# Five modulation rows moved into the up projection's loop, and a pause ahead of row 39

## The chip, the core and the metric

One core of a Trainium2 chip runs the whole kernel as one program. The core has a matrix engine (TensorE, PE in the profile, with its weight loads as PEld), a vector engine (VectorE, DVE), a scalar engine (ScalarE, ACT), GpSimd (POOL) and a queue that issues transfers (SyncE, SP); GpSimd issues transfers too. The metric is the device time of one execution, in us.

## The reference

Two groups of tokens go through one layer of a diffusion backbone: 128 context tokens and 512 latent tokens, 640 columns in all, with a model width of 1024.

```python
def trunk_layer(x, cvec, lw, ...):
    mod = jax.nn.silu(cvec) @ lw['w_ada'] + lw['b_ada']
    sh1, sc1, g1, sh2, sc2, g2 = jnp.split(mod, 6, axis=-1)
    h = rmsnorm(x, lw['norm1_g']) * (1.0 + sc1) + sh1
    mix, kh, vh, s_f, s_b = token_mixers(h, lw, ...)
    x = x + g1 * mix
    h = rmsnorm(x, lw['norm2_g']) * (1.0 + sc2) + sh2
    x = x + g2 * conv_ffn(h, lw['w_up'], lw['ffn_conv_w'], lw['ffn_conv_b'], lw['w_down'])

def conv_ffn(h, w_up, cw, cb, w_down):
    z = dwconv3(h @ w_up, cw, cb)
    a, g = jnp.split(z, 2, axis=-1)
    return (jax.nn.silu(g) * a) @ w_down
```

`mod` has 6 x 1024 entries for each of two condition vectors (c for the latent tokens, c_ctx for the context). In tiles of 128 these are 48 rows: 0 to 15 are sh1 and sc1, 16 to 23 g1, 24 to 39 sh2 and sc2, 40 to 47 g2. The token mixers hold a gated convolution, a recurrence, a neighbourhood attention over windows of keys with softmax, and a gated MLP.

## The kernel before

The program is one straight line of stages: the input projections (tile by tile, with the mixers' steps running beside them), the gates and branch products, the output projection, the second norm, the up projection (22 pairs of column tiles) and the down projection (42 units). Large products are made in float32 with a high and a low part of each operand, three matmuls of 320 columns for one, and with a Strassen-like scheme of seven products for a block of four.

**The modulation rows.** Rows 0 to 15 are made with matmuls at the start. The others are made on the vector engine without TensorE: a row's weights (128 x 1024, 512 KB from `w_adt`) are multiplied with silu(c) and silu(c_ctx), which stand spread over all partitions in the buffer S0, and summed along the row. `col_products` gives these two instructions (L285, one for each vector; the first writes its products to `junk`, the second over the weights). `modulate` (L234) or `gain_col` (L291) adds the bias. `ada_cols` is a job that does this for rows 16 to 41 beside the projections; it takes turns with the mixers' jobs by planned times, each `yield` naming planned us until its next step. Even rows are loaded into the buffer H, odd ones into X0 or A (in the attention's stage: A). The load of a row is asked for ahead of the products of the row before it, or behind its first product.

**The attention's stage.** `attn` goes over 16 units (head pair, column block, head) in rounds of two. `s1` makes the scores of two units on TensorE (L841, L844), adds bias and mask (L848), takes the maxima (L850), and ScalarE makes the exponentials (L851). `s2` scales by the reciprocal sums on the vector engine (L857, L858) and transposes the scores on TensorE (L861) into B (copied by the vector or the scalar engine). `s3` multiplies with the values (L878). Between these steps TensorE works on the input projection's tiles (L375). What stands in which order on each engine follows from the planned times; at run time each engine goes through its instructions in order.

**The up projection.** `up_all` calls `up_pair` for each pair p. Its instructions stand on each engine in the order of the code (`ovec`, `oact`, `opool` keep it). In a pair the vector engine does: the convolution's taps of an older pair, differences into `ubuf`, the low part of the next pair's first weights (`up_al`), `first_sum`, the gated product, the weight sums of the next pair (`up_sums`, out of the weights' buffers raw and G), taps, the last difference of the pair before, and low parts of the weight sums (`up_bl`). The weights of pair p+2 are asked for in pair p. TensorE makes seven products of 12 matmuls (L1512), 84 in a pair.

**The down projection.** `down_start(u)` opens unit u: it asks for parts of the activations that the up projection has left in memory (A, B, C, D, E, F), makes some of the modulation rows (`col_make` by the table `COLS`), and in unit 26 turns g2's columns into rows (`gain_rows`), which are read back into S0. `col_open`, behind the up loop, loads and activates the condition vectors again and asks for rows 42 and 43. Transfers made by `sync` keep the order in which the code asks for them.

The table of the rows in the down projection, and the settings of `ada_cols` (the last entry is the first row that it does not make):

```python
AE = (("fb", 1), 0.5, 0.5, 42)
...
COLS = dict(zip((23, 21, 19, 9, 6, 3), range(47, 39, -1)))
```

So before, rows 42, 43, 44, 45, 46 and 47 are made in units 3, 6, 9, 19, 21 and 23.

Of the kernel before, what the change touches and what calls it, by code (L numbers as in the profile page):

```python
# [12 lines left out]
AF = mybir.ActivationFunctionType  # L13
ALU = mybir.AluOpType
AX = mybir.AxisListType

P = 128
HY = 5
AE = (("fb", 1), 0.5, 0.5, 42)
COLWAIT = {}  # L20
HD = [4, 5, 2.1, 7, 2.2, 1.4, 1.5, 5, 2.0, 2, 11]
NPAIR = 22
NK = NPAIR // 2
BRIDGE = 4
# [26 lines left out]
D = 1024  # L51
# [10 lines left out]
C_C, C_BADA, C_N1, C_N2 = 0, 16, 64, 72  # L62
# [8 lines left out]
def tile_step(ctx: ExitStack, tc: tile.TileContext, a: dict, outs: list, dbg=None):  # L71
# [58 lines left out]
    def region(tag, shape, dt=F32):  # L130
        return big.tile(shape, dt, tag=tag, name=nm(tag))
# [24 lines left out]
    act, mm = Ordered(nc.scalar, boot).activation, ten.matmul  # L156
# [121 lines left out]
    def col_products(f, raw, cr):  # L278
        junk = gp.tile([P, D], mybir.dt.bfloat16, tag="gt", name=nm("junk"))
        ar = sp.tile([P, 2], F32, tag="red", name=nm("ar"))  # L280

        def steps():
            for v in range(2):
                tc.keep_in_program_order(
                    vec.scalar_tensor_tensor(raw if v else junk, raw, 1.0, cr[:, v], ALU.mult, ALU.mult,  # L285
                                             accum_out=ar[:, v:v + 1]))
                yield v
        return ar, steps()

    def gain_col(f, ar):  # L290
        vec.tensor_scalar(gcol[:, f // 8 // 5, :, f % 8], ar, p1[:, C_BADA + f:C_BADA + f + 1], None, ALU.add)  # L291

    def col_home(f):

# [1107 lines left out]
    def up_al(p_, raw):  # L1402
        w = up[p_, "A"]
        ovec.tensor_tensor(w[:, 2:4], raw, w[:, 0:2].bitcast(F32), ALU.subtract)
# [209 lines left out]
    def up_pair(p_, r):  # L1614


        n, q, o = p_ + 1, p_ - 1, p_ - 2
        inner, nx = p_ < NPAIR, n < NPAIR
        if p_ == 0:
            up_u2(p_)  # L1620
            up_back(1, "C", unit(1, 2), 5, 5, True)
            operand3()
        if o >= 0:
            taps(o, 1)
        if q >= 0:

            oact(tmp(2), up[q, "b"][0], AF.Copy)
            if p_ == 1:
                up_u2(p_)
            for (i0, i1, c) in S2:  # L1630
                ovec.tensor_tensor(ubuf(q, 1)[:, c:c + i1 - i0], up[q, "b"][1][:, i0:i1], tmp(2)[:, i0:i1],
                                  ALU.subtract)
        if nx and n >= BRIDGE:
            up_ah(n, r[n][0])
            up_al(n, r[n][0])
        if inner and p_ >= BRIDGE:
            up_start(p_)
            first_sum(p_)
        if o >= 0:
            gate(o)  # L1640
            gated(o)
        if nx and p_:
            up_sums(n, r[n], 0)
            up_sums(n, r[n], 1)
        elif p_ == NPAIR - 1:
            x_load("E")
            ld[UP + 2] = units[UP + 2][0]()
        if inner and p_ > 1:
            up_c(p_, r[p_])
        if o >= 0:  # L1650
            keep(o)
        if inner:
            if p_ + 2 < NPAIR:
                r[p_ + 2] = up_load(p_ + 2)
            elif p_ + 2 == NPAIR:
                ld[UP + 1] = units[UP + 1][0]()
        if q >= 0:

            c1 = up[q, "b"][0]
            prod(c1, q, 4, False)  # L1660
            for (i0, i1, c) in S2:
                oact(ubuf(q, 0)[:, c:c + i1 - i0], c1[:, i0:i1], AF.Copy)
            centre(q, 0)
            if p_ > 1:
                taps(q, 0)
        if inner and p_ > 1:
            up_u2(p_)
        if q >= 0:

            prod(up[q, "b"][1], q, 3, False)  # L1670
            ovec.tensor_tensor(ubuf(q, 1)[:, 1:1 + HC], up[q, "b"][1], tmp(q % 2), ALU.subtract)
            if p_ == 1:
                taps(q, 0)
                first_copy(3)
                first_sum(3)
        if nx and p_:
            up_b(n)
        if q >= 0:
            centre(q, 1)
        if nx and p_:  # L1680
            up_bl(n)
        if inner:
            b1, b2 = up[p_, "b"]
            prod(b2, p_, 5, True)
            prod(b1, p_, 7, False)
        if p_ == NPAIR - 1:
            x_load("C")
            rd[UP + 1] = units[UP + 1][1](ld[UP + 1])
            ld[UP + 3] = units[UP + 3][0]()
# [38 lines left out]
    def up_all(_):  # L1728
        fx["x"] = {1: (hh[0][:, 0], hh[0][:, 1]), 2: (hh[0][:, 2], hh[0][:, 3])}
        up_back(2, "A", unit(2, 0), 0, 4)  # L1730
        up_back(3, "A", unit(3, 0), 1, 4)
        up_back(0, "B", unit(0, 1), 2, 5)
        up_back(1, "B", unit(1, 1), 4, 5)
        drain(lambda: "n2_2" in R)
        for p_ in range(BRIDGE):
            up_start(p_)
            if p_ == 1:
                drain(lambda: "n2_3" in R)
                operands(0, 192)
        drain(lambda: "n2_4" in R)  # L1740
        r = {}
        up_back(0, "C", unit(0, 2), 3, 5)
        operands(192, HC)
        operands57()
        for p_ in range(NPAIR + 1):
            up_pair(p_, r)
        fixed[0] = False
        taps(NPAIR - 1, 1)
        gate(NPAIR - 1)
        gated(NPAIR - 1)  # L1750
        keep(NPAIR - 1)
        col_open()

    units.append((lambda: None, lambda pr: None, up_all))


# [18 lines left out]
    def x_load(tag, part=None):  # L1775

        if tag == "C":
            xr["C"] = region("C", [P, 2560])
            xr["p", 0] = xr["C"][:, 0:NK * P].rearrange("p (k t) -> p k t", t=P)
            sync(xr["p", 0], actp[0])  # L1780
            x_tail(0, 0)
        elif tag == "F":
            xr["F"] = region("F", [P, 2560])
            xr["p", 1] = xr["F"][:, D:D + NK * P].rearrange("p (k t) -> p k t", t=P)
            sync(xr["p", 1], actp[1])
            sync(xr["F"][:, 0:D], a["final_norm_g"].partition_broadcast(P))
        else:
            h, c = XR[tag]
            if (h, c) not in xr:
                xr[h, c] = region(tag, [P, 10, 256])  # L1790
            ks = slice(0, 10) if part is None else slice(5 * part, 5 * part + 5)
            sync(xr[h, c][:, ks], actx[h, c][:, ks])
            if part == 1:
                x_tail(h, c)

    def x_tail(h, c):
        o = NK * P + 256 * tail_of[h, c]
        xr["t", h, c] = xr["C"][:, o:o + 256].unsqueeze(1)
        sync(xr["t", h, c], actx[h, c][:, 10:11])
# [61 lines left out]
    hold = []  # L1861

    LAST = range(AE[3], 48)
    cols = {}

    def col_open():
        cols["c"] = region("S0", [P, 2, D])
        cf = cols["c"].rearrange("p v c -> p (v c)")
        sync(cf, a["cc"].rearrange("v c -> (v c)").partition_broadcast(P))
        keep_(act(cf, cf, AF.Silu))  # L1870
        for f in LAST[0:2]:
            col_load(f)

    def col_load(f):
        if f in LAST:
            cols[f] = region("HG"[f % 2], [P, D])
            sync(cols[f], a["w_adt"][f - 16])

    def col_make(f):
# [4 lines left out]
            pass  # L1884
        gain_col(f, ar[0])

    COLS = dict(zip((23, 21, 19, 9, 6, 3), range(47, 39, -1)))
    G2 = 27

    def down_start(u):  # L1890
        ph, j = DOWN[u]
        if u == 0:
            acc["b1"], acc["b2"] = [pm(), pm()], [pm(), pm()]
            g0, g1 = pg(), pg()
            acc["p"], acc["q"], acc["b3"] = g0[:, 0, :], g0[:, 1, :], [g1[:, 0, :], g1[:, 1, :]]
            r = region("XL1", [P, 5, 512])
            acc["c1"], acc["u2"], acc["cp"] = [r[:, 0], r[:, 1]], [r[:, 2], r[:, 3]], r[:, 4]
        for tag, part in {0: (("A", 0), ("B", 0)), 2: (("A", 1), ("B", 1)), 6: (("D", 0),), 8: (("D", 1),),
                          10: (("F", None),)}.get(u, ()):
            x_load(tag, part)  # L1900
        if u == 12:
            x2[2:4] = [x2r("X1")[:, 0:1024], x2r("X1")[:, 1024:2048]]
        if u - 2 in COLS:
            col_load(COLS[u - 2] + 2)
        if u in COLS:
            col_make(COLS[u])
        if u == G2 - 1:
            gain_rows(1)
        if u == G2:
            grows["g2"] = gain_load(1, "S0")  # L1910
            x2[4] = x2r("G")[:, 0:1024]
            r = region("H", [P, 2, 512])
            acc["u3"] = [r[:, 0], r[:, 1]]
        if u == 28:
            x2[0:2] = [x2r("X0")[:, 0:1024], x2r("X0")[:, 1024:2048]]
        for f in LATER.get((ph, j), ()):
            f()
# [493 lines left out]
```

## Time and profile before

| | us |
|---|---|
| runs: median of 3 (lowest, highest) | 1016.45 (1016.23, 1018.08) |
| the profiled execution's own time | 1015.32 |
| its span, first to last instruction | 1013.2 |
| busy: TensorE, vector engine, scalar engine, GpSimd | 993.9, 823.8, 559.4, 168.6 |
| attention's stage in the span | about 210 to 290 |
| up projection's loop | about 600 to 870 |
| down projection | about 866 to 1005, last matmul done at 1004.9 |

A line of a timeline has the start, the time, the engine, the source line, the operation, out<-in by the program's names and the shapes, a count, and in brackets how long the engine was idle ahead of it and what ended that. The page's slices are 25.3 us each; a digit is the busy share in tenths. A line of the waits names who waited, for whom, the us in total, how often, and the longest. A window's line gives the busy time and the number of instructions of each engine, the clock that was granted to TensorE, the share of the transfer engines that was busy, and GB/s.

### The profile page before, as it was taken

How to read it: one execution, taken by the hardware profiler on the slowest of the kernel's cores; microseconds unless marked ns; L12 is line 12 of the kernel's file. 1: busy time of each engine (PE TensorE's matmuls, PEld its weight loads, DVE VectorE, ACT ScalarE, POOL GpSimd, SP SyncE). 2: the span in 40 equal slices, each digit the busy share in tenths (PEclk: the TensorE clock that was granted, in tenths of full speed). 3: DMA queues.
4: the chain of work that ended last, by engine and by line, in shares of the span. 5: the costliest groups of instructions: out<-in, count | busy, mean ns of one | idle time of the engine just before them, and what ended most of it. 6: DMA issues, size and time to landing. Idle time of an engine off the chain costs nothing. (4 is left out here: it accounts for less than half of the span.)

```text
span 1013.2 us, 18951 instructions
## 1 busy us (share of the span) xinstructions
PE 993.9 (98%) x7503; PEld 941.4 (93%) x7503; DVE 823.8 (81%) x1381; ACT 559.4 (55%) x983; POOL 168.6 (17%) x223
## 2 busy tenths in 40 slices
PE   8999999997999999999999999999999999999996
PEld 6899999997999999999998899999999999888885
DVE  6778899867775667677778778998888887999897
ACT  6642343343464445444445376777777777756563
POOL 1000020322220122241010021222222222100013
PEclk9999999999999999999999999999999999999999
DMA  9875344596576399799249774766555666996462
GB/s 355 327 255 162 104 148 126 146 265 198 130 216 242 120 276 184 271 281 209 94 145 338 306 267 139 198 169 151 152 151 151 156 155 186 378 353 234 158 247 104
DMA packets 70010, 208.93 MB, mean 206 GB/s; under 512 B 9633, under 2 KB 24769, under 8 KB 67233
## 3 DMA queue, kind: packets, MB, share of 16 engines
q1 hardware_dynamic: 43536, 148.60, 41.2%
q0 software_dynamic: 26384, 59.12, 25.5%
q8 instruction: 59, 0.97, 0.4%
q14 instruction: 31, 0.25, 0.1%
HBM read 165.99 MB, written 48.51 MB: 212 GB/s over the span
## 5 line engine op out<-in xcount | busy, mean ns | idle before, releaser
L375 PE MATMUL g<-XH,w 128*128 128x320 f32 x704 | 171.7, 318 | 0.1
L375 PEld LDWEIGHTS g<-XH,w 128*128 128x128 f32 x704 | 121.2, 189 | 2.7 <-issue 1.0
L375 PE MATMUL g<-XL,w 128*128 128x320 f32 x352 | 109.0, 310 | 0.0
L375 PEld LDWEIGHTS g<-XL,w 128*128 128x128 f32 x352 | 66.6, 189 | 0.0
L1943 PE MATMUL m<-w,XH 128*128 128x512 f32 x246 | 58.6, 390 | 0.0
L1943 PEld LDWEIGHTS m<-w,XH 128*128 128x128 f32 x246 | 46.1, 188 | 9.7
L1152 PE MATMUL m<-XH,w 128*128 128x320 f32 x224 | 52.5, 309 | 0.0
L151 POOL DMA_DIRECT2D wsum<-in_w_dn_dram x36 | 36.5, 1154 | 53.0 <-issue 41.7
L151 ACT ACTIVATE w<-raw 128x1024 fp32r<-128x1024 f32 (+3 forms) x46 | 38.5, 852 | 2.3 <-DMA raw<-in_w_in_dram 1.1
L151 DVE SCALAR_TENSOR_TENSOR X<-MG,p2t,X 128x641 f32<-128x641 f32 x44 | 38.9, 884 | 1.1 <-ACT X L151 0.2
L151 DVE SCALAR_TENSOR_TENSOR X<-X,p2t,X 128x641 f32<-128x641 f32 x44 | 38.9, 884 | 1.0
L1512 PE MATMUL g<-XL,w 128*128 128x320 f32 x240 | 38.7, 310 | 0.0
L1152 PEld LDWEIGHTS m<-XH,w 128*128 128x128 f32 x224 | 38.3, 188 | 0.0
L1512 PE MATMUL g<-XL,C 128*128 128x320 f32 x240 | 38.3, 309 | 0.0
L1512 PEld LDWEIGHTS g<-XL,w 128*128 128x128 f32 x240 | 36.0, 188 | 0.6 <-ACT MG L151 0.3
L1512 PEld LDWEIGHTS g<-XL,C 128*128 128x128 f32 x240 | 36.0, 188 | 0.0
L1152 PE MATMUL m<-XL,w 128*128 128x320 f32 x112 | 34.6, 309 | 0.0
L151 ACT ACTIVATE ga<-m,cst 128x320 f32<-128x320 f32 x27 | 14.3, 528 | 36.6 <-PE m L1152 36.6
L151 DVE TENSOR_TENSOR w<-raw,w 128x1024 fp32r<-128x1024 f32 (+2 forms) x36 | 30.6, 871 | 2.5 <-ACT w L151 2.5
L151 ACT ACTIVATE X<-g 128x320 f32<-128x320 f32 x30 | 13.1, 437 | 34.6 <-PE g L1512 34.5
L1858 DVE TENSOR_TENSOR w<-raw,w 128x1024 fp32r<-128x1024 f32 (+1 forms) x26 | 30.1, 1156 | 2.5 <-ACT w L1854 2.5
L151 DVE TENSOR_TENSOR gb<-g,gb 128x640 f32<-128x640 f32 x12 | 9.9, 825 | 26.3 <-PE g L1165 25.4
(582 smaller groups left out, 2929.8 us busy)
## 6 DMA issues: line engine op xcount, KB each, us to landing
wsum<-in_w_dn_dram POOLq DMA_DIRECT2D x30, 512.0 KB, 11.7
raw<-in_w_up_dram SPq DMA_DIRECT2D x30, 512.0 KB, 5.5
raw<-in_w_gp_dram SPq DMA_DIRECT2D x21, 640.0 KB, 6.6
raw<-in_w_in_dram SPq DMA_DIRECT2D x19, 512.0 KB, 4.5
H<-in_w_adt_dram SPq DMA_DIRECT2D x16, 512.0 KB, 4.5
raw<-wsum SPq DMA_DIRECT2D x12, 512.0 KB, 5.3
actx<-X POOLq DMA_DIRECT2D x22, 256.0 KB, 4.4
wsum<-wsum POOLq DMA_DIRECT2D x10, 512.0 KB, 11.1
```

Of the source, the lines that this page charges most:

```text
L151: r = f(*args, **kw)
L375: mm(o, w[:, h, k0 + k, :], r(k)[:, s], start=(k == 0 and i == 0), stop=(k == kt - 1 and i == 2))
L1152: mm(o, w[:, k, :], x[:, k, :], start=(first and k == 0 and j == 0), stop=(k == 3 and j == 2), skip_group_check=True)
L1512: z = mm(o, w[:, k, :], x[:, k, :], start=(first and k == 0 and j == 0), stop=(k == 3 and j == 2), skip_group_check=True)
L1858: vec.tensor_tensor(w[:, 1, 0:n], raw, w[:, 0, 0:n].bitcast(F32), ALU.subtract)
L1943: mm(ps, s[t // 4][:, hx, k, o:o + P], w[:, hw, k, c0:c1], start=first, stop=i == 2 and bi == len(batch) - 1 and k == len(ks) - 1, skip_gr ...
```

## The change

`ada_cols` makes rows 16 to 39 only, and pauses for 8 planned us ahead of row 39. Rows 40 to 44 are made in the up loop: `up_row` puts one product into a pair, behind `up_al` and ahead of the pair's first products; a row's first product stands in pair 6, 9, 12, 15 or 18, its second with the bias in the pair after it. `col_open` moves from behind the loop to the start of pair 4, and the Silu of the condition vectors to pair 6. The next row's load is asked for behind a row's second product. Rows 45, 46 and 47 stay in units 19, 21 and 23 of the down projection. There, D is asked for in units 9 and 11 (was 6 and 8), F in 13 (was 10), a part of the second norm's input in 16 (was 12), and the last piece of B's part in 5 (was 2).

```diff
-AE = (("fb", 1), 0.5, 0.5, 42)
-COLWAIT = {}
+AE = (("fb", 1), 0.5, 0.5, 40)
+COLWAIT = {39: 8}
...
+        if p_ == BRIDGE:
+            col_open()
...
             up_al(n, r[n][0])
+            up_row(p_)
...
         keep(NPAIR - 1)
-        col_open()
...
-            if part == 1:
+            if part == 1 and tag != "B":
                 x_tail(h, c)
...
     LAST = range(AE[3], 48)
+    UPROWS = dict(zip((6, 9, 12, 15, 18), LAST))
     cols = {}
+
+    def up_row(p_):
+        if p_ in UPROWS:
+            f = UPROWS[p_]
+            if f == LAST[0]:
+                cf = cols["c"].rearrange("p v c -> p (v c)")
+                keep_(act(cf, cf, AF.Silu))
+            cols["job"] = (f,) + col_products(f, cols.pop(f), cols["c"])
+        if "job" in cols:
+            f, ar, steps = cols["job"]
+            if next(steps) == 1:
+                keep_(gain_col(f, ar))
+                del cols["job"]
+                if f + 1 in LAST:
+                    col_load(f + 1)

     def col_open():
         cols["c"] = region("S0", [P, 2, D])
         cf = cols["c"].rearrange("p v c -> p (v c)")
         sync(cf, a["cc"].rearrange("v c -> (v c)").partition_broadcast(P))
-        keep_(act(cf, cf, AF.Silu))
-        for f in LAST[0:2]:
-            col_load(f)
+        col_load(LAST[0])

     def col_load(f):
         if f in LAST:
-            cols[f] = region("HG"[f % 2], [P, D])
+            cols[f] = region("G" if f == 46 else "H", [P, D])
             sync(cols[f], a["w_adt"][f - 16])
...
-    COLS = dict(zip((23, 21, 19, 9, 6, 3), range(47, 39, -1)))
+    COLS = dict(zip((23, 21, 19), range(47, 44, -1)))
...
-        for tag, part in {0: (("A", 0), ("B", 0)), 2: (("A", 1), ("B", 1)), 6: (("D", 0),), 8: (("D", 1),),
-                          10: (("F", None),)}.get(u, ()):
+        for tag, part in {0: (("A", 0), ("B", 0)), 2: (("A", 1), ("B", 1)), 9: (("D", 0),), 11: (("D", 1),),
+                          13: (("F", None),)}.get(u, ()):
             x_load(tag, part)
-        if u == 12:
+        if u == 5:
+            x_tail(1, 1)
+        if u == 16:
             x2[2:4] = [x2r("X1")[:, 0:1024], x2r("X1")[:, 1024:2048]]
-        if u - 2 in COLS:
-            col_load(COLS[u - 2] + 2)
+        if u + 2 in COLS and COLS[u + 2] > 45:
+            col_load(COLS[u + 2])
```

On the vector engine in the attention's stage, before: row 38's end (modt), then row 39's first product (out of A), then the scaling of round 0's scores (ast holds the sums, X the scores, m a bank of TensorE's results).

```order
L234 TENSOR_SCALAR modt<-ar_2940,bada_240,cst 128x2
L285 SCALAR_TENSOR_TENSOR junk_2997,ar_2998<-A_2357,S_82_887 128x1024
L857 RECIPROCAL ast_2876<-ast_2876 128x1 x2
L858 TENSOR_SCALAR X_252_2814<-X_252_2814,ast_2876 128x384 x2
L848 TENSOR_TENSOR X_253_2815<-m_3007,B_2816 128x384
L848 TENSOR_TENSOR X_253_2815<-m_3009,B_2816 128x384
L850 TENSOR_REDUCE ast_2876<-X_253_2815 128x1 x2
L285 SCALAR_TENSOR_TENSOR A_2357,ar_2998<-A_2357,S_82_887 128x1024
```

The same place of the changed kernel, from row 38's end on:

```order
L234 TENSOR_SCALAR modt<-ar_2940,bada_240,cst 128x2
L857 RECIPROCAL ast_2876<-ast_2876 128x1
L858 TENSOR_SCALAR X_252_2814<-X_252_2814,ast_2876 128x384
L857 RECIPROCAL ast_2876<-ast_2876 128x1
L858 TENSOR_SCALAR X_252_2814<-X_252_2814,ast_2876 128x384
L848 TENSOR_TENSOR X_253_2815<-m_3002,B_2816 128x384
L848 TENSOR_TENSOR X_253_2815<-m_3004,B_2816 128x384
L850 TENSOR_REDUCE ast_2876<-X_253_2815 128x1 x2
```

And a little later, where row 39 now stands:

```order
L848 TENSOR_TENSOR X_252_2814<-m_3083,B_2816 128x384
L848 TENSOR_TENSOR X_252_2814<-m_3085,B_2816 128x384
L850 TENSOR_REDUCE ast_2876<-X_252_2814 128x1 x2
L285 SCALAR_TENSOR_TENSOR junk_3100,ar_3101<-A_2357,S_82_887 128x1024
L2137 COPY B_2816<-m_3111 128x384
L285 SCALAR_TENSOR_TENSOR A_2357,ar_3101<-A_2357,S_82_887 128x1024
```

Row 39's first product has moved from ahead of the scaling of the first round's scores to behind the maxima of the third round's, one scaling and two score rounds later. Rows 40 and 41, which followed it, are gone from this stage.

On the vector engine in the up loop, pair 7 of the changed kernel, around row 40's second product (MG<-raw is `up_al`, MG<-m,s is `first_sum`; before, these two stand next to each other):

```order
L151 TENSOR_TENSOR X_617_6754<-g_7311,X_616_6740 128x128
L151 TENSOR_TENSOR MG_663_7437<-raw_7354,MG_663_7437 128x1024
L285 SCALAR_TENSOR_TENSOR H_7039,ar_7309<-H_7039,S_635_7037 128x1024
L291 TENSOR_SCALAR gcol<-ar_7309,cst 128x2
L151 TENSOR_TENSOR MG_597_6559<-m_7459,s_666_7457 128x320
L151 TENSOR_TENSOR X_616_6740<-X_616_6740 128x641
```

A product, and in each second of these pairs the bias, now stand between the low part of the weights and `first_sum`.

On the SP queue of the changed kernel, row 41's load and its neighbours in the same pair (before, the weight loads follow each other without it):

```order
L1384 DMA raw_7356<-in_w_up_dram 128x1024
L1384 DMA raw_7487<-in_w_up_dram 128x1024
L1761 DMA H_7442<-in_w_adt_dram 128x1024
L1384 DMA G_7489<-in_w_up_dram 128x1024
L1384 DMA raw_7616<-in_w_up_dram 128x1024
```

The row's load has come between two halves of a pair's weights, so the second half's load and all later ones stand behind it. TensorE's own order is the same in both kernels but for two matmuls at one place in the bridge to the down projection.

More of the change, by code (lines that the diff above doesn't have):

```diff
@@ L290, in gain_col @@
     def gain_col(f, ar):
-        vec.tensor_scalar(gcol[:, f // 8 // 5, :, f % 8], ar, p1[:, C_BADA + f:C_BADA + f + 1], None, ALU.add)
+        return vec.tensor_scalar(gcol[:, f // 8 // 5, :, f % 8], ar, p1[:, C_BADA + f:C_BADA + f + 1], None, ALU.add)
     def col_home(f):
```

## The prediction

> **What bounds the kernel now.** I read the busy line and the slices of the page, then the waits of TensorE, then windows and timelines around the one wait that counts.
>
> ```profile
> PE 993.9 (98%) x7503; PEld 941.4 (93%) x7503; DVE 823.8 (81%) x1381; ACT 559.4 (55%) x983; POOL 168.6 (17%) x223
> PE   8999999997999999999999999999999999999996
> PE m L861 <- DVE X L858: 5.7, 1, 5.7
> DVE junk L285 <- DMA A<-in_w_adt_dram: 7.6, 1, 7.6
> ```
>
> TensorE is busy 993.9 of 1013.2 us, so 19.3 us are left. Between start and end only one slice is below 9, the tenth (228 to 253 us), and the third line is its cause: TensorE waited 5.7 us once, for the vector engine's softmax scaling (L858). The fourth says what the vector engine was doing then: it stood 7.6 us in front of a modulation product (L285) whose weight row had not landed. The timelines show both, with the load:
>
> ```profile
> 228.40 0.31 PE L375 MATMUL g<-XH,w 128*128 128x320 f32 x1
> 234.44 1.51 PE L861 MATMUL m<-cst,X 128*128 128x128 f32 x6 [5.73 <-DVE X L858]
> 242.64 0.82 PE L861 MATMUL m<-cst,X 128*128 128x128 f32 x6
> 249.55 0.82 PE L861 MATMUL m<-cst,X 128*128 128x128 f32 x6
> ...
> 224.69 0.28 DVE L234 TENSOR_SCALAR modt<-ar,bada,cst 128x2 f32<-128x2 f32 x1
> 232.53 1.23 DVE L285 SCALAR_TENSOR_TENSOR junk<-A,S 128x1024 bf16<-128x1024 f32 x1 [7.56 <-DMA A<-in_w_adt_dram]
> 233.68 0.22 DVE L857 RECIPROCAL ast<-ast 128x1 f32<-128x1 f32 x2
> 233.88 0.75 DVE L858 TENSOR_SCALAR X<-X,ast 128x384 f32<-128x384 f32 x2
> ...
> A<-in_w_adt_dram SPq DMA_DIRECT2D x1, 512.0 KB, 10.8
> ```
>
> Rows of w_adt go into H (even) and A (odd), so this A is row 39; the modt of 224.69 closes row 38. The load took 10.8 us to land and the vector engine, in order, could not start the scaling behind it. The scaling itself was ready: its exponentials had ended before 226 us (ACT row below). The windows show what went with the stall:
>
> ```profile
> core 0: us, PE busy (x) PEld busy (x) DVE busy (x) ACT busy (x) POOL busy (x), PEclk, DMA share, GB/s
> 225.00:228.50 3.50, 3.50 (x27) 3.08 (x25) 0.00 (x0) 2.23 (x6) 0.00 (x0) 1.00 0.99 348
> 228.50:234.50 6.00, 0.27 (x3) 0.09 (x2) 1.97 (x6) 0.14 (x1) 0.00 (x0) 0.94 0.91 356
> 234.50:237.50 3.00, 3.00 (x14) 3.00 (x15) 3.00 (x6) 1.45 (x5) 1.41 (x2) 0.55 0.02 7
> 242.60:249.60 7.00, 7.00 (x59) 6.46 (x58) 7.00 (x18) 3.86 (x8) 1.93 (x4) 1.00 0.67 188
> 640.00:850.00 210.00, 210.00 (x1434) 210.00 (x1433) 189.22 (x279) 152.66 (x263) 55.21 (x72) 1.00 0.63 159
> 900.00:925.00 25.00, 25.00 (x112) 20.69 (x111) 25.00 (x44) 13.66 (x21) 0.00 (x0) 1.00 0.91 337
> ```
>
> The transfers ran at 356 GB/s until the row landed, and after the wait the granted clock was 0.55 for three us. In the up projection (640 to 850) and the down projection (900 to 925) TensorE has no gap at all: there the other engines' loads are not the bound.
>
> **The pause ahead of row 39.** It takes row 39's first product from its place ahead of round 0's scaling to behind the maxima of the third score round. Nothing else moves ahead of the scaling, so the stall at L861 goes if the chain without row 39 is in time. For the stalled transposes it is:
>
> ```profile
> 225.53 0.19 ACT L851 ACTIVATION_READ_ACCUMULATOR X<-X,ast 128x1 f32 x1
> 225.93 0.39 PE L844 MATMUL m<-B,F 64*128 64x128 f32 x4
> 234.54 1.02 DVE L848 TENSOR_TENSOR X<-m,B 128x384 f32<-128x384 f32 x2
> 235.47 1.00 DVE L850 TENSOR_REDUCE ast<-X 128x1 f32<-128x384 f32 x2
> 240.91 0.39 PE L844 MATMUL m<-B,F 64*128 64x128 f32 x4
> 237.17 0.19 ACT L851 ACTIVATION_READ_ACCUMULATOR X<-X,ast 128x1 f32 x1
> ```
>
> The exponentials end at 225.72; reciprocals and scalings (0.22 and 0.75, some 0.95 back to back) give 226.7, and TensorE gets there at 228.7. Saved: 5.73 us. The wait also cost clock: from L861 to L861 a step takes 249.55 - 242.64 = 6.91 us, but the step behind the stall took 242.64 - 234.44 = 8.20, so 1.29 us more. In sum 7.0 us.
>
> The Trainium skill ("TensorE: Matmul & The Clock Gate", What's actually happening) says that an idle window of about 3.4 us drops the clock to half, and that a busy one of that length brings it back. The trace's 0.55 after a 5.73 us gap agrees in kind. By that rule a cold window would cost half of 3.4, 1.7 us as an estimate, and the sum would be 7.4 instead of 7.0; the measured 1.29 decides.
>
> What is late next? The following transposes come 6.91 us later, at 235.6. Their scores are out of TensorE at 226.3; sums and maxima (1.02 and 1.00) end at 228.3; the two exponentials ended 0.9 us behind their maxima (237.36 against 236.47), so at 229.2; the scalings at 230.2: 5.4 us to spare. Row 39 now stands behind the third round's maxima. Those scores ended at 241.3 and come 7.0 us earlier, at 234.3, so their maxima end at 236.3. The row landed at 232.5 in the old order, and the load of row 40, issued behind it, is gone. So 3.8 us to spare there, and I take the residual wait as zero. Its bounds are 0 and the whole 5.73.
>
> **Rows 40 and 41 leave the attention.** Four products and two loads fewer. The window 242.6 to 249.6 has the vector engine full (7.00 of 7.00) and TensorE full as well, so the relief is worth nothing to the end; it covers the products of row 39 that come into that stretch.
>
> **Rows 40 to 44 in the up loop.** One product per pair in pairs 6, 7, 9, 10 up to 19, on the vector engine's fixed order, between a pair's weight remainder and its first sum.
>
> ```profile
> 218.00 1.22 DVE L285 SCALAR_TENSOR_TENSOR junk<-H,S 128x1024 bf16<-128x1024 f32 x1
> 219.15 0.08 DVE L285 DVE_READ_ACCUMULATOR junk<-H,S 128x1 f32 x1
> 944.42 0.21 DVE L291 TENSOR_SCALAR gcol<-ar,cst 128x2 f32<-128x2 f32 x1
> ...
> 694.80 1.23 DVE L151 TENSOR_TENSOR w<-raw,w 128x1024 fp32r<-128x1024 f32 x1 [0.35 <-ACT w L151]
> 696.97 0.49 DVE L151 TENSOR_TENSOR MG<-m,s 128x320 f32<-128x320 f32 x1 [0.95 <-PE m L1512]
> 698.11 0.69 DVE L151 TENSOR_TENSOR F<-raw,G 128x512 f32<-128x512 f32 x1
> 702.37 0.48 DVE L151 TENSOR_TENSOR X<-g,X 128x320 f32<-128x320 f32 x1
> ...
> 705.50 1.92 PE L1512 MATMUL g<-XH,w 128*128 128x320 f32 x12
> 690.28 0.33 SPq L1384 DMA_DIRECT2D G<-in_w_up_dram  x1
> DMA to landing us min/median/max: 3.8/3.9/5.5
> ```
>
> A product takes 1.15 us of the queue (218.00 to 219.15), a second product with its gain 1.15 + 0.21 = 1.36. Exactly where it is put the vector engine waits 0.95 us for TensorE. So first_sum comes 0.20 us late in a pair with a first product and 0.41 in one with a second; at the next weight remainder 0.35 us of waiting are free, and each third pair has no product. The lag does not build up. What does TensorE need soonest from behind it? The bank pair that X<-g at 702.37 empties, done at 702.85, and TensorE writes it again at 705.50: 2.65 us against a lag of 0.41. Cost: none; at the other end, if every late first_sum reached TensorE, five times 0.20 + 0.41, 3.1 us. The opening Silu (1.90 us on the scalar engine in the old place) falls once into pair 6, where it delays that first_sum's copy by less than the same 2.65.
>
> The loads of rows 41 to 45 wait on the SP queue for the product that frees H, and the loads of the up weights stand behind them. That product comes at about the place of 696.97 in its pair; the G load behind it, issued at 690.28 when its buffer came free, belongs to the pair before the one of 696.97; a pair's 84 matmuls take 84 x 210/1434 = 12.3 us, so that pair's place is 684.7, 5.6 us ahead of the issue, and the row load holds nothing up. It lands in 3.9 (at most 5.5) and is read at 698.11, 7.83 after the issue: 2.3 to 3.9 us to spare. The Trainium skill ("DMA: Bandwidth & Descriptors", Queues, rings and completion order) says that each engine takes turns between the rows it has work for, packet by packet. By that, an estimate, the GpSimd transfer that frees G could take twice its time beside a row load, and the lag would grow by some tenths of a us. No row here shows the two together; it speaks for the second rival below.
>
> **Down projection.** Rows 42 to 44 leave units 3, 6 and 9, and the loads of D and F are asked for three units later. TensorE is full there (25.00 of 25.00), so the freed 3 x 2.51 = 7.5 us of the vector engine give nothing. The loads:
>
> ```profile
> 900.38 0.39 SPq L1760 DMA_DIRECT2D XL<-wsum  x1
> D<-actx SPq DMA_DIRECT2D x2, 640.0 KB, 6.3
> 929.25 2.88 PE L1943 MATMUL g<-MG,XH 128*128 128x512 f32 x12
> 1003.63 1.24 PE L1943 MATMUL m<-w,MG 128*128 128x256 f32 x9
> ```
>
> D now stands behind the weight load of 900.38 and lands near 908; its first products are those of 929.25. The stretch behind the last matmul, 1004.9 to 1013.2, is untouched.
>
> **The sum.** The profiled execution took 1015.3 us, 2.1 more than its span. Less 7.0 that is 1008.3. The median of the runs, 1016.45, stands 1.1 above it, so I forecast 1016.45 - 7.0 = 1009.4 us.
>
> **Rivals.**
> - Part of the stall comes back: row 39, or a transpose whose spare time I overrate, makes TensorE wait some 3 us a step or two later. For it: the vector engine was full in that stretch; against it: rows 40 and 41 are gone. A gap of 3 us leaves 4.0 saved, 1012.4; if it comes back whole (the pause then only carries the wait along), nothing is saved. By the Trainium skill's clock rule (the page named above) a gap under 3.4 us would cost no cold stretch on top. Chance 0.12, of which 0.03 for the whole.
> - Slower: in the up loop the vector engine becomes the bound. Five rows take 5 x (1.15 + 1.36) = 12.6 us; if all of it came onto TensorE's path the time is 1009.4 + 12.6 = 1022. It decides from a lag above 2.65 us on, and the kernel is slower once more than 7.0 of the 12.6 are exposed. For it: 189.22 of 210 us are busy there already. Against it: the free 0.95 + 0.35 us in each pair. Chance 0.07.
> - The later loads of D or F hold the down projection up. They would have to land some 20 us later than worked out; one exposed D load costs 6.3 us, 1015.7. Chance 0.03.
>
> **How the numbers follow.** The forecast has 0.78, the partial return 0.09, the whole one 0.03, the slower case 0.07, the late loads 0.03. A measurement of this kernel tells about 0.2%, 2 us, from no change. Faster: 0.78 + 0.09 = 0.87; within 0.2%: the whole return and the exposed D load, 0.06; slower: 0.07. The range reaches up to the partial return (1012.4) and the exposed first_sums (1009.4 + 3.1 = 1012.5), so to 1012.6. Downwards the fastest run of before, 1016.23, gives 1009.2; of TensorE's 19.3 idle us 5.7 go here and 8.3 lie behind the last matmul, and I leave one us of the other 5.3 for what the attention's relief may give: 1008.2.
>
> **What would show it.** Right: no wait of TensorE at L861, a granted clock of 1.00 from 225 to 240, L861 to L861 steps of 6.91 us from the first on; row 39's product starting without a DMA wait; in the up loop 1434 matmuls in 210 us as now, with first_sum's wait for TensorE gone in the pairs with a product; the last matmul 7 us earlier and the same 8.3 us behind it. Wrong: a DMA wait in front of row 39 at its new place, a gap in TensorE's row between 640 and 850, or a wait for D or F behind 920.

## The result, and the profile after

The changed kernel takes 1008.58 us (median of 4 runs, 1008.12 to 1009.04), the kernel before 1016.66 beside it (4 runs, 1016.23 to 1018.08): a ratio of 0.992, 95% interval 0.9904 to 0.9935. The forecast was 1009.4, range 1008.2 to 1012.6. The profiled execution took 1008.12 us, its span is 1006.0.

The page's busy line and TensorE's slices, then the longest row of TensorE's waits, of the changed kernel:

```profile
PE 993.2 (99%) x7503; PEld 941.0 (94%) x7503; DVE 825.0 (82%) x1381; ACT 558.5 (56%) x983; POOL 168.4 (17%) x223
PE   8999999999999999999999999999999999999996
PE g L151 <- DVE F L151: 1.6, 1, 1.6
```

The same work (993.2 us) stands in a span that is 7.2 us shorter. The 7 in the tenth slice is gone, and the longest wait that is left is one of 1.6 us, which the kernel before has as well. The windows over the place of the old stall, and the up projection:

```profile
228.50:234.50 6.00, 6.00 (x52) 5.47 (x50) 2.18 (x7) 2.88 (x8) 0.89 (x1) 1.00 1.04 334
234.50:237.50 3.00, 3.00 (x24) 2.99 (x23) 3.00 (x7) 1.78 (x6) 1.42 (x2) 1.00 0.24 46
640.00:850.00 210.00, 210.00 (x1434) 210.00 (x1433) 198.24 (x302) 151.43 (x259) 52.16 (x68) 1.00 0.66 178
```

TensorE is full at a clock of 1.00 where it stood for 5.73 us and then ran at 0.55. The up loop makes the same 1434 matmuls in 210 us, with 9 us more of work on the vector engine. Timelines of TensorE, the vector engine and SP around row 39:

```profile
228.50 0.82 PE L861 MATMUL m<-cst,X 128*128 128x128 f32 x6
...
235.40 0.82 PE L861 MATMUL m<-cst,X 128*128 128x128 f32 x6
...
242.31 0.82 PE L861 MATMUL m<-cst,X 128*128 128x128 f32 x6
...
225.90 0.42 DVE L858 TENSOR_SCALAR X<-X,ast 128x384 f32<-128x384 f32 x1
236.00 1.29 DVE L285 SCALAR_TENSOR_TENSOR junk<-A,S 128x1024 bf16<-128x1024 f32 x1
A<-in_w_adt_dram SPq DMA_DIRECT2D x1, 512.0 KB, 10.1
222.68 1.04 SPq L251 DMA_DIRECT2D A<-in_w_adt_dram  x1
```

The scaling of 225.90 no longer stands behind row 39. That row's load, issued at 222.68, lands 10.1 us later, at 232.8, and its product starts at 236.00 with no wait. The step from transposes to transposes is 6.9 us from the first on. Where the gain arises can be read off three landmarks of TensorE: the last start of L878 (the attention's products with the values), and the first and the last start of one form of L1512 (the up projection). Before, and then in the changed kernel:

```profile
L878 PE MATMUL m<-B,X x64: 272/273/324, 239.6 to 287.9; 128*64 128x128 f32 x64
L1512 PE MATMUL g<-XL,C x240: 309/309/309, 617.8 to 862.0; 128*128 128x320 f32 x120
```

```profile
L878 PE MATMUL m<-B,X x64: 272/273/323, 232.3 to 280.6; 128*64 128x128 f32 x64
L1512 PE MATMUL g<-XL,C x240: 309/309/309, 610.6 to 854.8; 128*128 128x320 f32 x120
```

So 7.3 us are won by the end of the attention, 7.2 at the up projection's start and 7.2 at its end. The last matmul ends at 997.6 instead of 1004.9, again 7.3. What lies behind the attention gives or takes nothing.

### The profile page after: what moved, and what is told of

The parts are those of the page before. It is cut to its first block, busy times and chain, and to the rows that moved or that the text cites. A ratio compares the mean times of both kernels' runs of the same rounds, so it can differ in the third digit from the quotient of the medians.

```text
span 1006.0 us, 18962 instructions
## 1 busy us (share of the span) xinstructions
PE 993.2 (99%) x7503; PEld 941.0 (94%) x7503; DVE 825.0 (82%) x1381; ACT 558.5 (56%) x983; POOL 168.4 (17%) x223
## 5 line engine op out<-in xcount | busy, mean ns | idle before, releaser
L1512 PE MATMUL g<-XL,w 128*128 128x320 f32 x240 | 38.6, 310 | 0.0
L1512 PE MATMUL g<-XL,C 128*128 128x320 f32 x240 | 38.3, 309 | 0.0
L1512 PEld LDWEIGHTS g<-XL,w 128*128 128x128 f32 x240 | 36.0, 188 | 0.6 <-ACT MG L151 0.3
L1512 PEld LDWEIGHTS g<-XL,C 128*128 128x128 f32 x240 | 36.0, 188 | 0.0
L336 ACT ACTIVATE w<-raw 128x1024 fp32r<-128x1024 f32 (+1 forms) x22 | 24.3, 1104 | 12.2 <-PE m L947 8.2
```

Source lines behind the costliest of these rows:

```text
L336: high = lambda: act(w[:, 0], raw, AF.Copy)
L1512: z = mm(o, w[:, k, :], x[:, k, :], start=(first and k == 0 and j == 0), stop=(k == 3 and j == 2), skip_group_check=True)
```

## Experiments

**The two halves alone.** The pause alone is the kernel before with `COLWAIT = {39: 8}`:

> The kernel before with the 8 us pause ahead of row 39 and nothing else; rows 40 and 41 stay in the attention's stage, 42 to 44 in the down projection. Theory (the whole gain is the stall of TensorE behind row 39, 5.7 us, and the low clock after it, 1.3 us): about 1009.5 us, L861 to L861 steps of 6.91 us. Rival (the gain needs rows 40 to 44 out of the attention and the down projection): 1013 to 1017 us.

Measured: 1010.55 us (1009.88 to 1011.30) against 1016.20, ratio 0.9945 (0.9931 to 0.9960). The rest is the changed kernel with `COLWAIT = {}`:

> The changed kernel without the pause. Theory: row 39 stands ahead of the scaling again and its load lands no earlier, so the stall of 5 to 6 us and the clock after it are back: about 1015.5 us. Rival (the move of the rows brings the gain, because row 40's load no longer crowds row 39's): 1009 to 1011 us.

Measured: 1016.99 us (1015.54 to 1018.81, 10 runs), ratio 1.0010 (1.0001 to 1.0019). The waits of TensorE in it:

```profile
PE m L861 <- DVE X L858: 6.0, 1, 6.0
```

The old stall stands whole, so moving the rows brings nothing by itself. But the pause alone is some 2 us short of the whole change (1007.8 us of span in its trace, against 1006.0): the two halves are worth more together than apart. TensorE of the pause alone runs within 0.2 us of the changed kernel up to 259 us, and then (TensorE, and the vector engine ahead of it):

```profile
260.61 0.94 PE L861 MATMUL m<-cst,X 128*128 128x128 f32 x6 [0.33 <-DVE X L858]
264.84 0.88 PE L861 MATMUL m<-cst,X 128*128 128x128 f32 x6
...
250.66 1.29 DVE L285 SCALAR_TENSOR_TENSOR junk<-A,S 128x1024 bf16<-128x1024 f32 x1
253.07 1.21 DVE L285 SCALAR_TENSOR_TENSOR A<-A,S 128x1024 f32<-128x1024 f32 x1
256.19 1.00 DVE L722 SCALAR_TENSOR_TENSOR MG<-MG,cst 128x511 f32<-128x511 f32 x2
260.14 0.74 DVE L858 TENSOR_SCALAR X<-X,ast 128x384 f32<-128x384 f32 x2
```

The pause pushes rows 40 and 41 along with row 39. Row 41's two products (2.5 us) now fall into the round in which the vector engine also does a convolution's taps (L718 to L722). That round's scaling is done only at 260.9. The planned order has laid its transposes behind that, at 260.61 where the changed kernel has them at 256.12, and from 262.2 on only the attention's own short matmuls stand between them and the next. The next transposes come at 264.84, in the changed kernel at 263.03: 1.8 us late, and the last start of L878 is 1.8 late as well (282.4 against 280.6). The trace calls only 0.33 us of this a wait. The attention's matmuls behind it take 2.64 us (262.20 to 264.84) where the changed kernel takes 1.66 (259.94 to 261.60); why they do is not shown.

**Is it the rows, or where row 41 stands?** Two kernels tell this apart: the pause alone with a second one, and the changed kernel with row 40 left in the attention.

```diff
-COLWAIT = {39: 8}                     # the pause alone
+COLWAIT = {39: 8, 41: 8}
```
```diff
-AE = (("fb", 1), 0.5, 0.5, 40)        # the changed kernel
+AE = (("fb", 1), 0.5, 0.5, 41)
-    UPROWS = dict(zip((6, 9, 12, 15, 18), LAST))
+    UPROWS = dict(zip((9, 12, 15, 18), LAST))
```

> The pause alone kept 1.7 us of what the whole change brings: up to 259 us its TensorE stands within 0.2 us of the changed kernel, and at 264.8 us it is 1.8 us late. Theory: row 41's product, put back by the pause into the round in which VectorE also does the convolution's taps, makes that round's second transposes late. A second pause of 8 ahead of row 41 takes the product behind the taps; rows 40 and 41 stay in the attention's stage. Theory: about 1008.8 us, no late transposes near 260 us, the up projection's first product of the pair form near 610.8 us as in the changed kernel (612.3 us with one pause). Rival: it is the presence of rows 40 and 41 in this stage (their loads and 5 us of VectorE) that costs, wherever they stand: 1010.5 us, 612.3 us.

> The changed kernel with row 40 left in the attention's stage and rows 41 to 44 in the up projection's loop. Theory (row 41's place among the taps was the 1.7 us): 1008.6 us, the same as the changed kernel within 0.5, no wait of TensorE between 243 and 265 us. Rival (each of the two rows costs its half where it stands): 1009.4 us.

Measured: 1008.38 us (1008.18 to 1009.21; ratio 0.9914, 0.9899 to 0.9929) and 1008.71 (1008.20 to 1008.82; ratio 0.9915, 0.9900 to 0.9929). Both are the whole gain. In the first, row 41's product has gone behind the taps and the transposes are at their times:

```profile
256.18 0.82 PE L861 MATMUL m<-cst,X 128*128 128x128 f32 x6
263.09 0.82 PE L861 MATMUL m<-cst,X 128*128 128x128 f32 x6
257.94 1.21 DVE L285 SCALAR_TENSOR_TENSOR junk<-A,S 128x1024 bf16<-128x1024 f32 x1
```

So it was row 41's place, not the two rows' loads or time. Two pauses with no row moved bring the whole gain, and no version that was run beats the changed kernel by more than the scatter.

**Without the load.** The kernel before, with row 39's load left out (its product reads what row 37 left in A, so the result is not the reference's), and no pause:

```diff
-                nc.sync.dma_start(raws[f], a["w_adt"][f - 16])
+                if f != 39:
+                    nc.sync.dma_start(raws[f], a["w_adt"][f - 16])
```

> The kernel before, with row 39's load left out: its two products stay in their old place and read what row 37 left in A, so that row's result is not the reference's. Theory (it is the lateness of the load, not the vector engine's time for the product): the scaling ends near 228 and TensorE comes at 228.5, so no stall: about 1009.5 us. Rival (the product's own time, or the vector engine's load in that stretch, holds TensorE): 1012 us or more.

Measured: 1008.83 us (1008.58 to 1009.10), ratio 0.9928 (0.9913 to 0.9943). Rows 39 and 40 on the vector engine (the inserted line makes L285 L286):

```profile
225.19 1.22 DVE L286 SCALAR_TENSOR_TENSOR junk<-A,S 128x1024 bf16<-128x1024 f32 x1
233.01 1.23 DVE L286 SCALAR_TENSOR_TENSOR junk<-H,S 128x1024 bf16<-128x1024 f32 x1 [2.00 <-DMA H<-in_w_adt_dram]
```

The product stands in its old place ahead of the scaling, takes its time and costs nothing: being rid of the late landing is worth what the change brings. (The edit also takes 512 KB of transfers out, which the pauses do not; they bring the same gain.) Here the vector engine even waits 2.00 us for row 40, and no wait of TensorE follows: here a wait on a transfer costs only what exceeds the spare time of the work behind it.

**Shorter pauses**, 2 and 4 instead of 8:

> The changed kernel with a pause of 2 instead of 8: row 39's first product stands ahead of the copy of the first transposed scores, one score round earlier than in the changed kernel. Theory: the vector engine gets there at 228.3 and waits for the row until 232.8; the copy ends near 234.5 where TensorE wants it at 232.3, so TensorE waits about 2.2 us, too short to lower the clock: about 1010.8 us and a granted clock of 1.00 behind the gap. If any gap lowers the clock: 1012 us. If the place of the product does not matter as long as the scaling is ahead of it: 1008.6 us.

> The changed kernel with a pause of 4 instead of 8: row 39's first product stands directly behind the first scaling and ahead of the second round's scores on the vector engine. Theory: it waits from 226.4 to 232.8; the second round's sums, maxima, then the copy of the first transposed scores follow, the copy ends near 237.2 where TensorE wants it at 232.3: a gap of about 4.9 us with the low clock behind it, 1008.6 + 4.9 + 1.3 = about 1014.8 us. If the place does not matter: 1008.6 us.

Measured: 1011.27 us (1010.00 to 1012.26; ratio 0.9949, 0.9933 to 0.9966) with 2, and 1016.33 (1015.30 to 1017.55, 10 runs; ratio 0.9993, 0.9984 to 1.0003) with 4. The longer of the two is the worse, and 1.5 us above what was expected. The vector engine's row 39 and TensorE's wait, with 2 and then with 4:

```profile
232.51 1.23 DVE L285 SCALAR_TENSOR_TENSOR junk<-A,S 128x1024 bf16<-128x1024 f32 x1 [4.14 <-DMA A<-in_w_adt_dram]
PE m L878 <- DVE B L2137: 1.8, 1, 1.8
```

```profile
232.39 1.22 DVE L285 SCALAR_TENSOR_TENSOR junk<-A,S 128x1024 bf16<-128x1024 f32 x1 [6.06 <-DMA A<-in_w_adt_dram]
PE m L878 <- DVE B L2137: 4.8, 1, 4.8
```

With 2 the product stands behind the second round's maxima and ahead of the copy of B; with 4, ahead of that round's scores and maxima. Why the longer planned pause puts it earlier in the order is not shown. Either way the wait of the vector engine ends with the landing, and what differs is how much work stands behind it. With 4 a wait of 4.8 us replaces the one of 5.7, and nothing is won. For the pause of 2 a clock of 1.00 had been expected after the gap; a window (TensorE alone) shows otherwise:

```profile
core 0: us, PE busy (x), PEclk, DMA share, GB/s
235.00:239.00 4.00, 4.00 (x22) 0.57 0.32 79
```

Its first L878 came 1.95 us later than the changed kernel's (234.27 against 232.32), its last 3.5 (284.1 against 280.6): the clock cost nearly as much again as the wait.

**More products in the up loop.** Each of the ten made twice, then three times (the extra sum goes to a spare column):

```diff
...
+            for _ in range(1):         # 2 for three times
+                o = raw if v else j
+                keep_(vec.scalar_tensor_tensor(o, raw, 1.0, cr[:, v], ALU.mult, ALU.mult, accum_out=st2[:, 7:8]))
...
```

> The changed kernel with each product in the up loop made twice (the second result unused). Theory (a pair has 1.30 us of free vector time, and TensorE notices a lag only above 2.65 us): five rows add 5 x 4.81 = 24.1 us, of which 14 pairs take 18.2 and the buffers 2.65, so about 3 us are exposed: about 1012 us. Rival (vector time in this loop is on TensorE's path, the rows are already paid for): five more rows cost 11.5 us: 1020 us. If the slack is larger than read: 1008.6 us.

> The changed kernel with each product in the up loop made three times. Theory: 5 x 7.11 = 35.6 us added, 18.2 + 2.65 of it covered, about 14.7 exposed: about 1023 us. Rival (all vector time is on the path): 1008.6 + 23 = 1032 us. If the slack is larger than read: 1012 us or less.

Measured: 1011.90 us (1011.63 to 1012.40; ratio 0.9952, 0.9937 to 0.9966) and 1023.71 (1023.44 to 1024.54; ratio 1.0069, 1.0052 to 1.0086). Windows of 640 to 740 in the changed kernel, twice and three times, and the largest wait of TensorE in the last (its L1513 is L1512 of the changed kernel):

```profile
640.00:740.00 100.00, 100.00 (x684) 100.00 (x683) 96.09 (x147) 74.17 (x127) 24.77 (x33) 1.00 0.68 186
```

```profile
640.00:740.00 100.00, 99.77 (x678) 99.24 (x678) 98.66 (x151) 72.58 (x124) 24.59 (x32) 1.00 0.68 186
```

```profile
640.00:740.00 100.00, 96.77 (x650) 95.08 (x650) 98.50 (x153) 68.71 (x120) 24.64 (x32) 1.00 0.65 175
PE g L1513 <- DVE X L151: 7.3, 5, 1.6
```

Ten products more (10 x 1.15 = 11.5 us) cost 3.3 us, the next ten 11.8, all of their time. So the loop had room for some 8 us (11.5 - 3.3) beyond the change's 12.6. The rival "the vector engine becomes the bound" comes true somewhere between the change's ten products and twenty.

**The later loads of the down projection.** All of them put back to their old units (D 6 and 8, F 10, X1 12, B's tail in 2):

> The changed kernel with the down projection's loads asked for where they were before (D in units 6 and 8, F in 10, the second norm's input in 12, the last piece of B's part in 2). Theory (TensorE is full there and every load is many us early): no difference, 1008.6 us within 1. Rival (with the rows gone, the new places bring part of the gain): 1010 us or more.

Measured: 1010.68 us (1009.28 to 1011.78), ratio 0.9938 (0.9923 to 0.9953): 2.1 over the changed kernel, a miss. SP's wait and timeline in it, then ScalarE's and TensorE's timelines:

```profile
SPq L1761 <- DMA actx<-X: 11.0, 1, 11.0
881.82 0.85 SPq L1761 DMA_DIRECT2D XL<-wsum  x2
...
885.93 1.06 ACT L1855 ACTIVATE MG<-XL 128x1024 fp32r<-128x1024 f32 x1 [1.74 <-DMA XL<-wsum]
889.44 2.48 PE L1958 MATMUL g<-w,MG 128*128 128x512 f32 x6 [1.86 <-ACT XL L1991]
```

SP stands 11.0 us in front of a small load whose data, the last pair's results, are still being stored. The loads of the summed weights (wsum) are queued behind it. ScalarE waits 1.74 us for one of them, and the evictions that TensorE needs (XL<-m, L1991) are queued behind that. Two kernels split the edits: the first has B's tail alone put back, the second everything but B's tail:

> The changed kernel with one load alone put back to its place before: the small load of B's tail, which then stands in SP's queue ahead of the first loads of wsum. With all the down projection's loads put back, 1010.68 us came instead of 1008.6, and in its trace SP stood 10.5 us ahead of that small load, the loads of wsum behind it went out at 881.8 us instead of 870.1, ScalarE waited 1.7 us for one of them and TensorE 1.9 us behind ScalarE. Theory: 1010.7 us (a wait of TensorE near 887 us and a stretch of clock 0.50 behind it). Rival (the places of D, F and X1 did it): 1008.6 us and no such wait.

> The counterpart: the loads of D, F and X1 at their places before, B's tail where the change puts it. Theory (the tail in front of wsum's loads was the cost): 1008.6 us, no wait of TensorE near 887 us. Rival (D, F and X1): 1010.7 us with that wait.

Measured: 1009.44 us (three runs at 1009.44 or 1009.45, one at 1012.83; ratio 0.9923, 0.9906 to 0.9939), and 1008.57 (1008.29 to 1009.92; ratio 0.9917, 0.9902 to 0.9932). The trace of the first is of the run at 1012.83. TensorE's wait for these evictions and SP's timeline in it, and below in the second:

```profile
PE g L1958 <- ACT XL L1991: 2.2, 1, 2.2
881.30 0.85 SPq L1761 DMA_DIRECT2D XL<-wsum  x2
```

```profile
PE g L1960 <- ACT XL L1993: 0.3, 1, 0.3
871.02 5.89 SPq L1761 DMA_DIRECT2D XL<-wsum  x2
```

In the changed kernel wsum is asked for at 870.05. So the stall comes and goes with the tail's place, and the places of D, F and X1 cost nothing while the tail stands late. How much the tail's place costs from run to run is not shown: 1010.7 was expected for the tail alone and 1009.44 came, only 0.9 over the changed kernel. The traced run has the stall (and a second wait of 1.0 us later), and its span is 5.0 us longer; the other three runs have no trace. Whether the old places of D, F and X1 add to the cost beside an early tail is open too. The kernel before had SP's wait as well (8.8 us) and no stall from it:

```profile
890.70 1.28 ACT L1976 ACTIVATE XL<-m 128x512 f32<-128x512 f32 x2 [0.49 <-PE m L1943]
892.87 1.06 ACT L1854 ACTIVATE MG<-XL 128x1024 fp32r<-128x1024 f32 x1
```

There the evictions (XL<-m) stand ahead of the split of the summed weights into high and low part (MG<-XL), so a late wsum could not hold them up; nor does the split wait here.

## Why the prediction was right, point by point

- **The stall and its price: right.** 7.2 us of the span went where the sum said 7.0 would. The medians differ by 8.1. The sum was made against an execution of 1015.32, 1.1 below its own median, and the forecast took the same 7.0 off the median; runs of before scatter over 3 us, those of the changed kernel over 0.9. That the forecast hit within a microsecond is in part luck within this scatter. The stall was 5.73 us in the trace of before and 6.0 in that of the rows alone: that the scatter comes from the landing of row 39's load is likely, and not shown run by run.
- **What is late next: right.** Row 39's product stands at 236.00 (236.3 forecast), its row lands at 232.8 (232.5): 3.2 us to spare, not 3.8.
- **Rows 40 and 41 "worth nothing": the step that failed.** It asked what the relief brings in the old order, and there the answer holds (the rows moved without the pause: 1016.99). It did not ask where the pause would push these rows. With the pause and without the move the kernel loses 1.8 us by 265 us. That is the first rival, the partial return, by another row than the one it named; the move of row 41 took it out. Total and chances came out because both halves were made.
- **The up loop: right, but for the first row.** Measured against pair 8, which has no product, and with 12.32 us to a pair, row 40's two pairs have `first_sum` 0.78 and 0.70 us late (665.89 and 678.13 against 689.75), where the prediction had 0.20 and 0.41. The first of these pairs holds the Silu, for which the product waited 0.30, and the pair ahead of it was late already, in the kernel before too. Row 41's pairs are 0.11 and 0.37 us late (702.18 and 714.76), and the rows behind it alike. All of this is far below the 2.65 us from which TensorE would notice, and TensorE has no gap there. As forecast, the wait for TensorE ahead of `first_sum` is gone in the pairs with a product and stands in the pairs without one. The row loads hold nothing up, as forecast: between 640 and 850 neither TensorE nor the vector engine nor ScalarE waits for a transfer.

```profile
664.74 1.23 DVE L285 SCALAR_TENSOR_TENSOR junk<-H,S 128x1024 bf16<-128x1024 f32 x1 [0.30 <-ACT S L1873]
665.89 0.49 DVE L151 TENSOR_TENSOR MG<-m,s 128x320 f32<-128x320 f32 x1
678.13 0.49 DVE L151 TENSOR_TENSOR MG<-m,s 128x320 f32<-128x320 f32 x1
689.75 0.49 DVE L151 TENSOR_TENSOR MG<-m,s 128x320 f32<-128x320 f32 x1 [0.70 <-PE m L1512]
...
702.18 0.49 DVE L151 TENSOR_TENSOR MG<-m,s 128x320 f32<-128x320 f32 x1
714.76 0.48 DVE L151 TENSOR_TENSOR MG<-m,s 128x320 f32<-128x320 f32 x1
```

- **The down projection: right for D and F, one edit overlooked.** The prediction costed the later loads of D and F and gave B's tail no line. It is the one that mattered: at its old place it brought a stall of about 2 us and a stretch at the low clock in the two traces of the changed kernel with the tail put back. That the change moved it was luck as far as the forecast goes. Behind the last matmul 8.4 us are left (8.3 before).

## What to carry to other kernels

An in-order engine that stands before a late transfer makes everything behind it late, so look at what is queued there, not at the waiting instruction: the same landing, at 232.4 to 232.8, cost 7.2 us of the traces' spans, 3.7, or nothing, by which steps stood behind it. Moving one step of a job moves the job's later steps too; follow each of them to its new neighbours. A queue that issues transfers is such an engine as well: here a small load that had to wait 10 to 11 us held up large ones that need not have waited.

## What the runs showed of the hardware

A gap of TensorE of 1.81 us (the pause of 2) or 1.86 us (the loads put back) was enough for the low clock, as 4.79 (the pause of 4) and 5.73 (before) were; gaps of 0.33 us (the pause alone) and 0.28 us (everything but B's tail put back) were not. A window of the kernel with the loads put back, one of the kernel before, and three short ones of the pause of 2:

```profile
890.00:894.00 4.00, 4.00 (x12) 0.58 1.01 406
```

```profile
233.00:238.00 5.00, 3.56 (x17) 0.66 0.17 70
```

```profile
234.00:235.00 1.00, 0.73 (x12) 1.00 1.08 209
236.00:237.00 1.00, 1.00 (x8) 0.50 0.02 4
239.00:240.00 1.00, 1.00 (x11) 1.00 0.94 367
```

Short windows show 0.50 in these stretches and 1.00 ahead of and behind them, in the other two kernels as well, so the low part lasts 4 x (1 - 0.58) / 0.50 = 3.4 us with the loads put back, 5 x (1 - 0.66) / 0.50 = 3.4 us in the kernel before, and 4 x (1 - 0.57) / 0.50 = 3.4 us in the pause of 2. At half the clock it costs up to half of that, 1.7 us as an estimate from these windows. It was about 1.5 in the pause of 2 (3.5 less 1.95), and 1.29 in the kernel before, where part of it fell into the gap itself. The Trainium skill ("TensorE: Matmul & The Clock Gate", What's actually happening) gives the window as about 3.4 us, which these runs bear out, and calls for an idle window of that length, which they do not: gaps of half that length took the clock down. The prediction's sentence that a gap under 3.4 us would cost no cold stretch is contradicted by the gaps of 1.81 and 1.86 us.
